# A hybrid attention and Fourier encoder layer: weight folds on another engine, one maximum for all late weights, squares and norms in another order

## The chip, the core and the metric

The kernel runs on one core of a Trainium2 chip. The core has five engines that run side by side, each through its own instructions in order: TensorE (PE, with its weight loads PEld), VectorE (DVE), ScalarE (ACT), GpSimd (POOL) and SyncE (SP, which here only issues DMA transfers). The metric is the device time of one launch in microseconds, the median over several runs.

## The reference, cut to what matters

One encoder layer, applied with the same weights to two requests (`prompt`, `sample`) of 2048 tokens with 1024 features:

```python
u = _rmsnorm(h, g_norm)
q, k, v, ga, f, gf = split(u @ w_in)          # 512, 128, 128, 512, 512, 512 columns
q = rope(_rmsnorm(q, g_q)); k = rope(_rmsnorm(k, g_k))        # per head of 64
a  = softmax(q k^T / 8) v * silu(ga)          # 8 query heads, 2 key/value heads, all tokens
fo = (Re(fft2(f)) per group of 64 channels, @ w_fmix) * silu(gf)
h = h + concat(a, fo) @ w_out
gate = sigmoid(_rmsnorm(h, g_ple) @ w_ple_gate)
y = _rmsnorm(h + (p @ w_ple) * gate, g_final)
```

All of it is float32. The kernel multiplies in float16, each operand split in a high and a low half, three products for one.

## The kernel before, in words

**Stages.** First the projections (`project`): x is read in 32 tiles of 128 rows, two tiles to a step, so 16 steps or chunks, 8 for each request. A row tile is scaled by its inverse norm, split in halves and transposed by DMA to `uc`. From it come q and kv (`mm_tile`), and, in the "sweep" of the chunk, f, gf and ga (`sweep_f`, `sweep_ga`). Then attention with the second half of the Fourier branch and the output projections beside it; the change does not touch the instructions of that stage, except for the order in which its first inputs are loaded and the place of its first maxima.

**The order of work is written out by hand.** Each engine gets its instructions in the order in which the program emits them. `iteration(i)` is the body of the projection: at its top the stores of the iteration before, then squares of the rows of chunk i+3 (`sq_u`, ACT, line 640, into `jk`), squares of z (q and k as projected) of chunk i-1 (`square_z`), the low halves of q of chunk i-3 (`lo_q`), the rotary product of chunk i-2 (`rope_q`), and `newton`: one inverse square root on DVE for q's norms of chunk i-1 and the row norms of chunk i+2 together (`rsqrt`, lines 269 to 284). Then the first row tile of chunk i, then the sweep of chunk i-1 in pieces (`sweep_part(us)` emits sweep steps until so many microseconds of PE work are spent). Between the pieces stand `fold_u`, `fold_s` (POOL, lines 811 and 817) and `fold_hl` (ACT and DVE, lines 824 and 825), which add and subtract the two row tiles of a chunk so that one matmul group does for both; behind the sweep stand `norm_q` (POOL, lines 627, 729 and 734), the high and low halves of u of chunk i+2 (`hi_u`, `lo_u`, and the transposes, line 481), the second half of the x loads for chunk i+4 (`load_x`, line 633, into 5 buffers), `hi_q` and the second row tile of chunk i.

**In a sweep**, f goes to PSUM, ACT copies it to `ft` (line 1004), and PE multiplies it by the first Fourier matrix (line 1009) between the two groups of gf. The results of gf, ga and the transform are stored by DMAs that POOL issues (lines 1052, 1071, 1018).

**Weights.** `weights` prepares the columns of q, kv, f, gf and ga at the start: load, maximum of each slice (DVE, line 349), maximum over the partitions (POOL, `partition_all_reduce`, line 359), a power of two as the factor, then the high and low halves (ACT and DVE, lines 371 and 372). For f, `fold_cols` first folds the columns of each of the 8 slices (POOL, lines 324 to 326). `weight_far` does the same for the weights of the output stage, six blocks, one after the other, with the halves going to DRAM; it runs as a background job, one turn for every five sweep steps (`bg`), and is followed in that job by `embed_rows`, which prepares p, and `channel_map`.

**The start of attention.** `early()`, at the end of iteration 13, loads the first k, v and q; `leads` then computes the first score maxima (lines 1325 and 1333), one turn for every five sweep steps.

Of the kernel before, what the change touches and what calls it, by code (L numbers as in the profile page):

```python
# [165 lines left out]
class Build:  # L166
# [151 lines left out]

    def fold_cols(self, w):

        g = self.nc.gpsimd
        e = w[:, :EVEN].rearrange("p (h c) -> p h c", c=33)[:, :, 1:32]
        o = w[:, EVEN:].rearrange("p (h c) -> p h c", c=31)
        g.tensor_tensor(out=e, in0=e, in1=o, op=ALU.add)
        g.tensor_scalar(out=o, in0=o, scalar1=-2.0, scalar2=None, op0=ALU.mult)
        g.tensor_tensor(out=o, in0=o, in1=e, op=ALU.add)

    def weights(self, blocks, stage, ahead):

        nc, st = self.nc, self.st
        sl = {}

        def load(i):
            if i < 8 * len(blocks):
                _, src, cols, _, _ = blocks[i // 8]
                sl[i] = stage(i % 8, cols)
                nc.sync.dma_start(sl[i], src[i % 8 * 128:(i % 8 + 1) * 128, :])
                if blocks[i // 8][0] == "f":  # L340
                    self.fold_cols(sl[i])

        for i in range(ahead):
            load(i)
            yield "loaded" if i == 7 else 0.0
        for b, (name, src, cols, g, dest) in enumerate(blocks):
            mx = st.tile([128, 8], F32, name="w_mx")
            for k in range(8):
                nc.vector.tensor_reduce(out=mx[:, k:k + 1], in_=sl[8 * b + k], op=ALU.max, axis=AX.X,
                                        apply_absolute_value=True)  # L350
                yield 0.0
            if g is not None:
                m2 = st.tile([128, 8], F32, name="w_m2")
                nc.vector.tensor_tensor(out=m2[:], in0=mx[:], in1=g[:], op=ALU.mult)
                mx = m2
            m1 = st.tile([128, 1], F32, name="w_m1")
            nc.vector.tensor_reduce(out=m1[:], in_=mx[:], op=ALU.max, axis=AX.X, apply_absolute_value=True)
            mm = st.tile([128, 1], F32, name="p2_mm")
            nc.gpsimd.partition_all_reduce(mm[:], m1[:], 128, bass_isa.ReduceOp.max)
            yield 0.0  # L360
            s, i = self.pow2_all("w_" + name, mm, W_EXP)
            self.sc[name] = i
            if g is not None:
                gs = st.tile([128, 8], F32, name="w_gs")
                nc.vector.tensor_scalar(out=gs[:], in0=g[:], scalar1=s[:], scalar2=None, op0=ALU.mult)
            dest = dest()
            yield 0.0
            for k in range(8):
                w = sl.pop(8 * b + k)
                f = gs[:, k:k + 1] if g is not None else s[:]  # L370
                nc.scalar.activation(dest[:, 0, k, :], w, AF.Copy, scale=f)  # L371
                nc.vector.scalar_tensor_tensor(out=dest[:, 1, k, :], in0=w, scalar=f, in1=dest[:, 0, k, :],  # L372
                                               op0=ALU.mult, op1=ALU.subtract)
                del w
                load(8 * b + k + ahead)
                yield "split" if k == 7 else 0.0

    def weight_far(self, name, src, cols, g, pool):

        nc, st = self.nc, self.st  # L380
        sl, ahead, nk = {}, AH, src.shape[0] // 128

        def load(j):
            if j < 2 * nk:
                sl[j] = pool.tile([128, 512], F32, name="w_st", tag="w2k", bufs=self.nw2k)
                nc.sync.dma_start(sl[j][:, :cols], src[j % nk * 128:(j % nk + 1) * 128, :])

        for j in range(ahead):
            load(j)
            yield  # L390
        mx = st.tile([128, 8], F32, name="w_mx")
        for k in range(nk):
            load(k + ahead)
            self.defer(lambda w=sl.pop(k), k=k: nc.vector.tensor_reduce(
                out=mx[:, k:k + 1], in_=w[:, :cols], op=ALU.max, axis=AX.X, apply_absolute_value=True))
            yield
        f = [None] * nk
        mm = st.tile([128, 1], F32, name="p2_mm")

        def scale():  # L400
            m = mx
            if g is not None:
                m = st.tile([128, 8], F32, name="w_m2")
                nc.vector.tensor_tensor(out=m[:], in0=mx[:], in1=g[:], op=ALU.mult)
            m1 = st.tile([128, 1], F32, name="w_m1")
            nc.vector.tensor_reduce(out=m1[:], in_=m[:, :nk], op=ALU.max, axis=AX.X, apply_absolute_value=True)
            nc.gpsimd.partition_all_reduce(mm[:], m1[:], 128, bass_isa.ReduceOp.max)

        def factors():
            s, self.sc[name] = self.pow2_all("w_" + name, mm, W_EXP)  # L410
            f[:] = [s[:]] * nk
            if g is not None:
                gs = st.tile([128, 8], F32, name="w_gs")
                nc.vector.tensor_scalar(out=gs[:], in0=g[:], scalar1=s[:], scalar2=None, op0=ALU.mult)
                f[:] = [gs[:, k:k + 1] for k in range(nk)]

        self.defer(scale)
        self.wd[name] = nc.dram_tensor("wd_" + name, (128, 2, nk, cols), F16, kind="Internal").ap()
        for _ in range(2):
            yield  # L420
        self.defer(factors)
        yield
        for k in range(nk):
            load(k + nk + ahead)
            w = sl.pop(k + nk)
            o = pool.tile([128, 2, 512], F16, name="w_o", tag="w2k", bufs=self.nw2k)
            nc.scalar.activation(o[:, 0, :cols], w[:, :cols], AF.Copy, scale=f[k])

            def low(k=k, w=w, o=o):
                nc.vector.scalar_tensor_tensor(out=o[:, 1, :cols], in0=w[:, :cols], scalar=f[k], in1=o[:, 0, :cols],  # L430
                                               op0=ALU.mult, op1=ALU.subtract)
                nc.sync.dma_start(self.wd[name][:, :, k, :], o[:, :, :cols])

            self.defer(low)
            yield

    def embed_rows(self, pool):
# [166 lines left out]
    def project(self, P, PU, W, early, later, wkv, wq, wf, wgf, wga, bg, mid):  # L604
# [241 lines left out]
        def iteration(i):  # L846
# [6 lines left out]
            for f in stores:  # L853
                f()
            del stores[:]
            if ok(i + 3):
                sq_u(i + 3)
            sq = square_z(i - 1) if ok(i - 1) else None
            if ok(i - 1) and i > 2:
                VL.pop((i - 1, 1))()  # L860
# [9 lines left out]
            if ok(i):  # L870
                sweep_part(4.0)
                VL.pop((i, 0))()
            if folds(i):
                sweep_part(1.5)
                fold_u(i, 0)
                fold_s(i, 0)
                fold_u(i, 1)
                sweep_part(8.0)
                fold_hl(i, 0)
                fold_s(i, 1)  # L880
                sweep_part(8.0)
                fold_hl(i, 1)
            sweep_part(1000.0 if i < n else (6.0, 9.0, 5.0, 100.0)[i - n])
            if ok(i - 1):
                norm_q(i - 1, rs)
            if ok(i + 2):
                hi_u(i + 2)
                for tt in range(CH):
# [5 lines left out]
            if ok(i):  # L894
                mm_tile(i, 1)
                append(i)
            if i == n - 3:
                early()
            if i == n:
# [67 lines left out]
        for f in stores_next:  # L967
            f()
        del stores_next[:]
        sq_u(3)  # L970
        sweep_part(11.6)
        mid()
        fold_u(1, 0)
        make_u(3, 0)
        load_x(5, 1)
        sq_u(4)
        fold_s(1, 0)
        fold_u(1, 1)
        sweep_part(3.0)
        fold_hl(1, 0)  # L980
        fold_s(1, 1)
        sweep_part(6.0)
        fold_hl(1, 1)
# [265 lines left out]
    def attention(self, kvp):  # L1249
# [7 lines left out]
        kt, vt, Q, P, O, MX, ACC, AT, M4, S, MR, AR = ({} for _ in range(12))  # L1257

        def load_kv(s, kv):
            for b in range(2):  # L1260
                k = kvp.tile([128, 4, 3, 128], F16, name=f"k{kv}", bufs=2)
                for h in range(2):
                    nc.sync.dma_start(k[:, 2 * h:2 * h + 2], self.kTd[s][kv][:, 4 * b + 2 * h:4 * b + 2 * h + 2])
                kt[s, kv, b] = k
            if s or not kv:
                load_v(s, kv)

        def load_v(s, kv):
            for b in range(2):
# [123 lines left out]

        self.kvp = kvp
        for kv in range(2):
            load_kv(0, kv)
            load_q(kv)
        nm = kvp.tile([128, 4, 128], F16, name="nm", bufs=1)
        nc.gpsimd.memset(nm[:], 0.0)
        kone = kvp.tile([128, 128], F16, name="kone", bufs=1)  # L1400
# [8 lines left out]
                negate(v - 1)  # L1409

        def leads():
            for g in range(-AHEAD, 0):
                yield from lead(g)
                yield
# [403 lines left out]
    def run(self):  # L1818
# [5 lines left out]
        with pool("psA", 5, space=PSUM) as self.psX, pool("A", side="right") as A:  # L1824
            with pool("A1", side="right") as A1:
# [58 lines left out]
                                   places([("uc", 3, 4), ("qs", 1, 2)] + [("qT", 2, 1)] * 2), 8)  # L1884

                def rest():
                    for n in range(2):
                        c = slice(n * 512, (n + 1) * 512)
                        yield from self.weight_far(f"wo{n}", a["w_out"][0][:, c], 512, None, A1)
                        yield from self.weight_far(f"pg{n}", a["w_ple_gate"][0][:, c], 512, self.gp, A1)  # L1890
                        yield from self.weight_far(f"wp{n}", a["w_ple"][0][:, c], 512, None, A1)
                    yield from self.embed_rows(A1)
                    yield from self.channel_map(A1)
                    self.scales3()
# [117 lines left out]
```

## Time and profile before

| | us |
|---|---|
| median of 3 runs | 2737.63 (2734.76 to 2737.71) |
| the profiled execution | 2728.66, span 2726.9 |
| granted PE clock, mean over the span | 0.974 |
| PE busy | 2536.3 (93%) |
| DVE busy | 1745.7 (64%) |
| ACT busy | 1182.6 (43%) |
| POOL busy | 1920.6 (70%) |
| projections, from the start to the first scores of attention | 863.7 |

How to read a row of the groups or the timeline: start and busy time, engine, line of the kernel, operation, output and inputs by the program's names, shape, count; in brackets the idle time of the engine before it and what ended it. A row of the waits gives the total, the number and the longest of the waits of one engine and line for another. "issue" as a releaser means that the profile shows nothing that the engine waited for. A name followed by q (SPq) is the engine's queue, which issues DMAs.

### The profile page before, as it was taken

How to read it: one execution, taken by the hardware profiler on the slowest of the kernel's cores; microseconds unless marked ns; L12 is line 12 of the kernel's file. 1: busy time of each engine (PE TensorE's matmuls, PEld its weight loads, DVE VectorE, ACT ScalarE, POOL GpSimd, SP SyncE). 2: the span in 40 equal slices, each digit the busy share in tenths (PEclk: the TensorE clock that was granted, in tenths of full speed). 3: DMA queues.
4: the chain of work that ended last, by engine and by line, in shares of the span. 5: the costliest groups of instructions: out<-in, count | busy, mean ns of one | idle time of the engine just before them, and what ended most of it. 6: DMA issues, size and time to landing. Idle time of an engine off the chain costs nothing. (4 is left out here: it accounts for less than half of the span.)

```text
span 2726.9 us, 49881 instructions
## 1 busy us (share of the span) xinstructions
PE 2536.3 (93%) x19896; PEld 1377.5 (51%) x19896; DVE 1745.7 (64%) x2326; ACT 1182.6 (43%) x1983; POOL 1920.6 (70%) x1598
## 2 busy tenths in 40 slices
PE   3898999979897999999999999999999999999998
PEld 1465656556555654444445454544444445544543
DVE  4767766767865675666566566665665566666634
ACT  2434324333322544544444445444444444544442
POOL 3255553545535996888788788888887887888870
PEclk7999999989898999999999999999999999999999
DMA  5646657657636762223232324322322222232223
GB/s 140 178 123 180 190 148 207 171 136 167 176 115 188 244 207 81 69 57 69 67 78 48 81 54 99 100 67 57 77 70 74 71 64 79 69 88 73 70 53 85
DMA packets 450601, 297.92 MB, mean 109 GB/s; under 512 B 294000, under 2 KB 394736, under 8 KB 450368
## 3 DMA queue, kind: packets, MB, share of 16 engines
q1 hardware_dynamic: 438512, 257.00, 36.9%
q0 software_dynamic: 11856, 37.74, 3.8%
q8 instruction: 155, 2.54, 0.4%
q14 instruction: 78, 0.64, 0.1%
HBM read 146.12 MB, written 82.45 MB: 84 GB/s over the span
## 5 line engine op out<-in xcount | busy, mean ns | idle before, releaser
L1303 POOL TENSOR_TENSOR acc<-acc,p 128x1024 f32<-128x1024 f32 x384 | 928.4, 2418 | 140.8 <-ACT p L1298 108.6
L1333 DVE TENSOR_REDUCE a_mx<-ps_m 128x1 f32<-128x1024 f32 x498 | 608.9, 1223 | 558.3 <-PE ps_m L1325 547.6
L1298 ACT ACTIVATE p<-ps_s,s_scale 128x512 f32<-128x512 f32 x1024 | 648.0, 684 | 668.1 <-PE ps_s L1295 650.9
L1619 PE MATMUL ps_g<-w_pg,hT 64*128 64x512 f16 x2784 | 494.9, 376 | 0.5 <-DVE h L1545 0.5
L1361 PE MATMUL ps_o<-p,v 128*64 128x256 f32 x4096 | 468.5, 382 | 0.0
L1295 PE MATMUL ps_s<-q,k 64*128 64x512 f16 x3072 | 435.7, 377 | 14.5 <-ACT p L1298 14.1
L488 PEld LDWEIGHTS <-uc 128*128 128x128 f16 x2400 | 239.8, 100 | 267.3 <-issue 64.0
L1361 PEld LDWEIGHTS ps_o<-p,v 128*64 128x64 f32 x4096 | 283.9, 137 | 160.0 <-issue 28.3
L1619 PEld LDWEIGHTS <-hT 64*128 64x128 f16 x2784 | 203.9, 94 | 156.4 <-issue 11.6
L1619 PE MATMUL ps_g<-w_wo,mh 64*128 64x512 f16 x1440 | 260.0, 376 | 13.7 <-DVE mh L1529 12.4
L1295 PEld LDWEIGHTS <-k 64*128 64x128 f16 x3072 | 151.9, 94 | 214.6 <-issue 93.5
L1619 PE MATMUL ps_g<-w_wo,mT 64*128 64x512 f16 x1440 | 259.2, 378 | 1.1 <-DMA mT<-mh 1.1
L1325 PE MATMUL ps_m<-k,q 64*128 64x512 f16 x996 | 201.2, 377 | 14.4 <-DVE a_mx L1333 14.4
L1301 POOL TENSOR_TENSOR acc<-p,p 128x1024 f32<-128x1024 f32 x64 | 150.9, 2358 | 25.6 <-ACT p L1298 24.8
L488 PEld LDWEIGHTS <-w_ga 128*128 128x128 f16 x1536 | 148.9, 98 | 26.5 <-DVE w_ga L372 3.7
L1619 PEld LDWEIGHTS <-mh 64*128 64x128 f16 x1440 | 100.6, 94 | 104.8 <-DVE mh L1529 17.6
L1619 PEld LDWEIGHTS <-mT 64*128 64x128 f16 x1440 | 103.7, 94 | 82.7 <-issue 5.1
L488 PE MATMUL ps_x<-w_gf,uc 128*128 128x512 f16 x552 | 135.0, 404 | 0.0
L1071 POOL DMA_DIRECT2D agd<-gat x64 | 35.4, 553 | 115.4 <-DVE gat L1081 104.1
L488 PE MATMUL ps_x<-wr_q,uc 128*128 128x512 f16 x384 | 88.0, 387 | 29.7 <-ACT wr_q L371 29.5
L488 PE MATMUL ps_x<-uc,w_ga 128*128 128x256 f16 x1008 | 113.5, 273 | 0.0
L1384 DVE RECIPROCAL ps_f<-ps_f 128x256 f32<-128x256 f32 x61 | 107.1, 1756 | 9.1 <-PE ps_f L1377 9.1
(342 smaller groups left out, 3464.0 us busy)
## 6 DMA issues: line engine op xcount, KB each, us to landing
q<-qTd SPq DMA_DIRECT2D x256, 64.0 KB, 2.3
ag<-agd SPq DMA_DIRECT2D x64, 256.0 KB, 3.2
out<-h POOLq DMA_DIRECT2D x31, 512.0 KB, 3.0
x<-in_x_prompt SPq DMA_DIRECT2D x16, 512.0 KB, 4.9
gfd<-gt POOLq DMA_DIRECT2D x32, 256.0 KB, 3.1
w_st<-in_w_out SPq DMA_DIRECT2D x32, 256.0 KB, 4.0
agd<-gat POOLq DMA_DIRECT2D x64, 128.0 KB, 2.8
w_st<-in_w_ple_gate SPq DMA_DIRECT2D x32, 256.0 KB, 3.7
```

The lines of the kernel that those rows point to most:

```text
L488: self.nc.tensor.matmul(ps, lhs(ia, k), rhs(ib, k), start=(i == 0), stop=(i == 3 * ks - 1))
L1071: nc.gpsimd.dma_start(self.agd[s][1, r * 128:(r + 1) * 128, c * n:(c + 1) * n], gt[:, :n])
L1295: nc.tensor.matmul(S[u][e][:], w[sl], q[sl].rearrange("p h q -> p (h q)"), start=j == i == 0, stop=i + 1 == len(todo), skip_group_check=True)
L1298: nc.scalar.activation(p[:, e, :], S[u][e][:], AF.Exp, scale=self.sc["s_scale"][:])
L1301: nc.gpsimd.tensor_tensor(out=ACC[u][:], in0=P[u, 0][:], in1=p[:], op=ALU.add)
L1303: nc.gpsimd.tensor_tensor(out=ACC[u][:], in0=ACC[u][:], in1=p[:], op=ALU.add)
L1325: nc.tensor.matmul(ps[c], Q[u][0][sl, h, :], kt[s, kv, half][sl, :, 0, :], start=True, stop=True)
L1333: nc.vector.reduce_max(MX[u][:, h, half, c:c + 1], x, axis=AX.X)
L1361: nc.tensor.matmul(o[64 * f:64 * f + 64], vt[s, kv, c // 8][:, c % 8, :], p[:, e, f], start=(c == 0), stop=(c == 15))
L1384: nc.vector.reciprocal(r, r)
L1619: nc.tensor.matmul(g[0][:], g[1](ia, k)[sl], g[2](ib, k)[sl], start=a, stop=z, skip_group_check=True)
```

## The change

Six edits, made together:

- `fold_cols` runs on VectorE, with two instructions for a slice instead of three, and is called just before the maximum of the slice and not when the slice is loaded.
- Behind ga's maximum over partitions GpSimd gets one small addition, whose result is not used.
- The six calls of `weight_far` become one `weights_far`: the maxima of all 36 slices first, one maximum over partitions for six columns, then all 36 splits.
- `sq_u(i+3)` moves from the top of `iteration(i)` to its end.
- `norm_q(i-1)` moves from behind the sweep to ahead of u's folds; the pieces of the sweep between them change a little. In the part before the loop, the first half of chunk 1's fold moves ahead of the squares and of `mid`.
- The first k and q tiles are loaded ahead of v, and `leads` waits four turns before it begins.

```diff
     def fold_cols(self, w):
-        g = self.nc.gpsimd
+        g = self.nc.vector
...
         g.tensor_tensor(out=e, in0=e, in1=o, op=ALU.add)
-        g.tensor_scalar(out=o, in0=o, scalar1=-2.0, scalar2=None, op0=ALU.mult)
-        g.tensor_tensor(out=o, in0=o, in1=e, op=ALU.add)
+        g.scalar_tensor_tensor(out=o, in0=o, scalar=-2.0, in1=e, op0=ALU.mult, op1=ALU.add)
...
     def weights(self, blocks, stage, ahead):
...
-                if blocks[i // 8][0] == "f":
-                    self.fold_cols(sl[i])
...
             for k in range(8):
+                if name == "f":
+                    self.fold_cols(sl[8 * b + k])
                 nc.vector.tensor_reduce(out=mx[:, k:k + 1], in_=sl[8 * b + k], op=ALU.max, axis=AX.X,
...
             nc.gpsimd.partition_all_reduce(mm[:], m1[:], 128, bass_isa.ReduceOp.max)
+            if name == "ga":
+                nc.gpsimd.tensor_tensor(out=m1[:], in0=m1[:], in1=mm[:], op=ALU.add)
...
-    def weight_far(self, name, src, cols, g, pool):
+    def weights_far(self, specs, pool):
...
+        for j in range(AH):
+            load(j)
+            yield
+        mx = pool.tile([128, n, 8], F32, name="w_mxs", bufs=1)
+        nc.vector.memset(mx[:], 0.0)
+        for j, (w, k) in enumerate(slices):
+            load(j + AH)
+            nc.vector.tensor_reduce(out=mx[:, w, k:k + 1], in_=sl.pop(j)[:], op=ALU.max, axis=AX.X,
+                                    apply_absolute_value=True)
+            yield
...
+        nc.vector.tensor_reduce(out=m[:], in_=mx[:], op=ALU.max, axis=AX.X, apply_absolute_value=True)
+        nc.gpsimd.partition_all_reduce(mm[:], m[:], 128, bass_isa.ReduceOp.max)
+        for _ in range(6):
+            yield
...
+        for j, (w, k) in enumerate(slices):
+            load(j + len(slices) + AH)
+            x = sl.pop(j + len(slices))
+            o = pool.tile([128, 2, 512], F16, name="w_o", tag="w2k", bufs=self.nw2k)
+            nc.scalar.activation(o[:, 0, :], x[:], AF.Copy, scale=f[w, k])
+            nc.vector.scalar_tensor_tensor(out=o[:, 1, :], in0=x[:], scalar=f[w, k], in1=o[:, 0, :],
+                                           op0=ALU.mult, op1=ALU.subtract)
+            nc.sync.dma_start(self.wd[specs[w][0]][:, :, k, :], o[:])
             yield
...
         def iteration(i):
...
-            if ok(i + 3):
-                sq_u(i + 3)
             sq = square_z(i - 1) if ok(i - 1) else None
...
                 sweep_part(4.0)
                 VL.pop((i, 0))()
+                sweep_part(4.0)
+            if ok(i - 1):
+                norm_q(i - 1, rs)
             if folds(i):
-                sweep_part(1.5)
                 fold_u(i, 0)
                 fold_s(i, 0)
                 fold_u(i, 1)
                 sweep_part(8.0)
                 fold_hl(i, 0)
                 fold_s(i, 1)
-                sweep_part(8.0)
+                sweep_part(7.0)
                 fold_hl(i, 1)
             sweep_part(1000.0 if i < n else (6.0, 9.0, 5.0, 100.0)[i - n])
-            if ok(i - 1):
-                norm_q(i - 1, rs)
...
                 mm_tile(i, 1)
                 append(i)
+            if ok(i + 3):
+                sq_u(i + 3)
...
+        fold_u(1, 0)
+        fold_s(1, 0)
+        sweep_part(5.8)
+        fold_hl(1, 0)
         sq_u(3)
-        sweep_part(11.6)
+        sweep_part(5.8)
         mid()
-        fold_u(1, 0)
         make_u(3, 0)
+        fold_u(1, 1)
         load_x(5, 1)
         sq_u(4)
-        fold_s(1, 0)
-        fold_u(1, 1)
-        sweep_part(3.0)
-        fold_hl(1, 0)
         fold_s(1, 1)
         sweep_part(6.0)
         fold_hl(1, 1)
...
         for kv in range(2):
-            load_kv(0, kv)
+            load_k(0, kv)
             load_q(kv)
+        load_v(0, 0)
...
         def leads():
+            for _ in range(4):
+                yield
             for g in range(-AHEAD, 0):
```

More of the change, by code (lines that the diff above doesn't have):

```diff
@@ L376, in weights @@
                 yield "split" if k == 7 else 0.0
-    def weight_far(self, name, src, cols, g, pool):
+    def weights_far(self, specs, pool):
         nc, st = self.nc, self.st
-        sl, ahead, nk = {}, AH, src.shape[0] // 128
+        n = len(specs)
+        slices = [(w, k) for w, (_, src, _) in enumerate(specs) for k in range(src.shape[0] // 128)]
+        sl = {}
         def load(j):
-            if j < 2 * nk:
+            if j < 2 * len(slices):
+                w, k = slices[j % len(slices)]
@@ L385, in load @@
                 sl[j] = pool.tile([128, 512], F32, name="w_st", tag="w2k", bufs=self.nw2k)
-                nc.sync.dma_start(sl[j][:, :cols], src[j % nk * 128:(j % nk + 1) * 128, :])
-        for j in range(ahead):
+                nc.sync.dma_start(sl[j][:], specs[w][1][k * 128:(k + 1) * 128, :])
+        for j in range(AH):
             load(j)
             yield
[L391 to L395, printed above, removed]
+        mx = pool.tile([128, n, 8], F32, name="w_mxs", bufs=1)
@@ L396, in weight_far @@
+        nc.vector.memset(mx[:], 0.0)
[3 more added lines that the diff above has]
+                                    apply_absolute_value=True)
             yield
[L397 to L401, printed above, removed]
+        for w, (_, _, g) in enumerate(specs):
             if g is not None:
[L403 to L407, printed above, removed]
@@ L409, in factors @@
-        def factors():
-            s, self.sc[name] = self.pow2_all("w_" + name, mm, W_EXP)
-            f[:] = [s[:]] * nk
-            if g is not None:
[L413 to L418, printed above, removed]
@@ L419, in weight_far @@
-        for _ in range(2):
-            yield
-        self.defer(factors)
+                nc.vector.tensor_tensor(out=mx[:, w], in0=mx[:, w], in1=g[:], op=ALU.mult)
+        m, mm, p = [st.tile([128, n], F32, name=f"wf_{x}", bufs=1) for x in ("m", "mm", "p")]
+        nc.vector.tensor_reduce(out=m[:], in_=mx[:], op=ALU.max, axis=AX.X, apply_absolute_value=True)
+        nc.gpsimd.partition_all_reduce(mm[:], m[:], 128, bass_isa.ReduceOp.max)
+        for _ in range(6):
+            yield
+        s, i = self.keep("wf_s", [128, n]), self.keep("wf_i", [128, n])
@@ new lines, in weights_far @@
+        nc.vector.tensor_scalar(out=p[:], in0=mm[:], scalar1=1e-30, scalar2=None, op0=ALU.max)
+        nc.vector.tensor_scalar(out=p[:].bitcast(I32), in0=p[:].bitcast(I32), scalar1=0x7F800000,
+                                scalar2=None, op0=ALU.bitwise_and)
+        nc.vector.tensor_scalar(out=s[:].bitcast(I32), in0=p[:].bitcast(I32), scalar1=-1,
+                                scalar2=(254 + W_EXP) << 23, op0=ALU.mult, op1=ALU.add)
+        nc.vector.tensor_scalar(out=i[:], in0=p[:], scalar1=2.0 ** -W_EXP, scalar2=None, op0=ALU.mult)
@@ new lines, in weights_far @@
+        f = {}
+        for w, (name, src, g) in enumerate(specs):
+            self.sc[name] = i[:, w:w + 1]
+            nk = src.shape[0] // 128
+            self.wd[name] = nc.dram_tensor("wd_" + name, (128, 2, nk, 512), F16, kind="Internal").ap()
+            for k in range(nk):
+                f[w, k] = s[:, w:w + 1]
+            if g is not None:
+                gs = pool.tile([128, 8], F32, name="w_gs8", bufs=2)
+                nc.vector.tensor_scalar(out=gs[:], in0=g[:], scalar1=s[:, w:w + 1], scalar2=None, op0=ALU.mult)
+                for k in range(nk):
+                    f[w, k] = gs[:, k:k + 1]
@@ L422, in weight_far @@
         yield
-        for k in range(nk):
-            load(k + nk + ahead)
-            w = sl.pop(k + nk)
+        for j, (w, k) in enumerate(slices):
+            load(j + len(slices) + AH)
+            x = sl.pop(j + len(slices))
             o = pool.tile([128, 2, 512], F16, name="w_o", tag="w2k", bufs=self.nw2k)
[L427 to L434, printed above, removed]
+            nc.scalar.activation(o[:, 0, :], x[:], AF.Copy, scale=f[w, k])
+            nc.vector.scalar_tensor_tensor(out=o[:, 1, :], in0=x[:], scalar=f[w, k], in1=o[:, 0, :],
+                                           op0=ALU.mult, op1=ALU.subtract)
+            nc.sync.dma_start(self.wd[specs[w][0]][:, :, k, :], o[:])
@@ L1259, in load_kv, with load_k @@
         def load_kv(s, kv):
+            load_k(s, kv)
+            load_v(s, kv)
+        def load_k(s, kv):
             for b in range(2):
@@ L1264, in load_kv @@
                 kt[s, kv, b] = k
-            if s or not kv:
-                load_v(s, kv)
         def load_v(s, kv):
@@ L1886, in rest @@
                 def rest():
[L1887 to L1891, printed above, removed]
+                    c = [slice(n * 512, (n + 1) * 512) for n in range(2)]
+                    yield from self.weights_far([x for n in range(2) for x in (
+                        (f"wo{n}", a["w_out"][0][:, c[n]], None), (f"pg{n}", a["w_ple_gate"][0][:, c[n]], self.gp),
+                        (f"wp{n}", a["w_ple"][0][:, c[n]], None))], A1)
                     yield from self.embed_rows(A1)
```

## The prediction

> **What bounds the kernel now.** First the busy time by stretch, then what TensorE (PE) waited for, then the timeline at those waits. In windows: length, busy time of PE, PEld, DVE, ACT, POOL, then the granted clock.
>
> ```profile
> 128.00:149.00 21.00, 8.84 (x51) 6.16 (x52) 9.70 (x19) 6.97 (x13) 16.73 (x15) 0.67 0.67 180
> 150.00:700.00 550.00, 508.98 (x3343) 331.47 (x3341) 400.74 (x701) 197.56 (x346) 282.91 (x232) 0.96 0.61 163
> 700.00:865.00 165.00, 138.51 (x866) 84.99 (x865) 118.81 (x236) 43.63 (x83) 76.95 (x70) 0.90 0.57 151
> ```
>
> Attention starts at about 864 and its instructions are not edited, so everything is decided before. There PE is the bound, with holes: 12.2 us in the first window (21.00 - 8.84), 41.0 in the second, 26.5 in the third. The waits of the first 1000 us name them, and a larger one at the start (total, times, longest):
>
> ```profile
> PE ps_x L488 <- ACT wr_q L371: 29.5, 1, 29.5
> PE ps_f L1009 <- ACT ft L1004: 16.5, 3, 7.2
> PE ps_g L1009 <- ACT ft L1004: 15.5, 1, 15.5
> PE ps_x L1325 <- DVE a_mx L1333: 13.1, 2, 6.7
> PE ps_g L1036 <- ACT uf L824: 11.2, 1, 11.2
> PE ps_x L1325 <- DMA q<-qTd: 10.7, 1, 10.7
> PE ps_x L1009 <- ACT ft L1004: 9.1, 2, 5.9
> ```
>
> The three ft rows are 41.1: all the idle time of 150 to 700. The Fourier transform (L1009) needs ft, and ACT is late with it. The timeline shows why, in program order:
>
> ```profile
> 232.96 4.70 SPq L481 DMA_TRANSPOSE uc<-hl  x2
> 237.71 0.96 SPq L633 DMA_DIRECT2D x<-in_x_prompt  x1
> 242.13 1.06 ACT L640 ACTIVATE jk<-x 128x1024 f16<-128x1024 f32 x1 [8.22 <-DMA x<-in_x_prompt]
> 245.28 0.70 ACT L1004 ACTIVATE ft<-ps_g,inv_f 128x512 f32<-128x512 f32 x1
> 246.04 2.08 PE L1009 MATMUL ps_f<-ft,dft 128*128 128x512 f32 x2 [7.24 <-ACT ft L1004]
> 247.91 4.29 PE L488 MATMUL ps_x<-w_gf,uc 128*128 128x512 f16 x10
> 640.02 1.02 PE L1009 MATMUL ps_x<-ft,dft 128*128 128x512 f32 x2
> 640.88 5.34 PE L488 MATMUL ps_x<-w_gf,uc 128*128 128x512 f16 x24
> ...
> 682.55 1.02 PE L1009 MATMUL ps_g<-ft,dft 128*128 128x512 f32 x2
> ```
>
> SP issues the row load at 237.71, once its transposes are out; ACT's next instruction squares those rows and stands 8.22 us; all of ACT's evacuations stand behind it. PE then starts cold: 2.08 against 1.02 for the transform, and 4.29 for ten matmuls that take 2.2 warm (5.34 x 10/24), so 3.1 us on top of the hole.
>
> **The change, part by part.**
>
> *Squares at the iteration's end.* `sq_u(i+3)` moves past everything ACT has in iteration i. Its rows were loaded at the end of iteration i-1, a whole iteration (over 40 us) earlier. It issues no DMA.
>
> ```profile
> ACT jk L640 <- DMA x<-in_x_sample: 61.0, 8, 11.1
> ACT jk L640 <- DMA x<-in_x_prompt: 12.4, 2, 8.2
> ACT uf L824 <- POOL f_s L817: 32.0, 8, 10.2
> ```
>
> Between 150 and 700 that takes 73.4 us of standing out of ACT. What it leaves behind: two squares of 1.06 in front of the squares of z, ready rows, nothing late. Worth on PE: the 41.0 of holes and the cold starts. Five holes at about 3 us each are 14, so 55 is there. An undisturbed chunk, transform to transform, is 42.5 us of back-to-back PE (640.02 to 682.55), so no other engine forbids it: DVE's 400.74 of 550 and POOL's 282.91 leave room.
>
> *norm_q before u's folds.* Now POOL folds u while DVE's Newton steps run, and `norm_q` follows at the end, beside DVE's split of u:
>
> ```profile
> 7.46 0.18 DVE L274 TENSOR_TENSOR rsq_t<-rsq_y 128x22 f32<-128x22 f32 x1
> 571.43 0.71 POOL L627 TENSOR_TENSOR rt<-rt,g_q_t 128x256 f32<-128x256 f32 x1 [7.48 <-issue]
> 572.91 2.33 POOL L729 TENSOR_TENSOR qn<-z,q_rs 128x1280 f32<-128x1280 f32 x1
> 575.32 3.47 POOL L734 TENSOR_TENSOR t<-qn,rt 128x1024 f32<-128x1024 f32 x2
> 583.86 2.06 DVE L274 TENSOR_TENSOR rsq_t<-rsq_y 128x22 f32<-128x22 f32 x1
> 593.25 0.91 ACT L468 ACTIVATE p_hl<-p_in,p_f 128x256 f16<-128x256 f32 x2 [15.57 <-DVE p_f L463]
> ```
>
> An operation of 0.18 takes 2.06 beside POOL's fold, and the wait of 15.57 behind it made the 15.5 hole. After the change POOL cannot start `qn` before Newton ends, so Newton runs free. In exchange folds queue behind 7.2 us (0.71 x 2 + 2.33 + 3.47), and the gfd, gd and agd stores POOL issues stand behind both. My estimate from these rows and the order of instructions, counted from the end of PE's previous row tile: squares and sums to 8, Newton to 12, norm_q to 18, f_t and f_s to 23; ACT reaches its first uf at about 25 (8 of row tile, 16 of sweep). About 2 us of slack. If that goes, the row above says what covers it: ACT waited for f_s eight times, up to 10.2, and PE never for that in 150 to 700, since its banks are ahead. SP: the rope load, issued at an iteration's top, is now needed some 25 us sooner, but still after Newton.
>
> *One maximum over partitions.* Six all-reduces become one; each made POOL switch code, 7.48 us before L627 after one of them (row above) and as much in front (5.98 below). Five less free POOL of some 65 us (5 x 13.5), and its norm_q at 571.43 comes on time. The same 72 loads and 36 stores stay; the background job has 21 turns fewer (102 to 81), so p's loads and transposes reach SP about 105 sweep steps (five to a turn), over one chunk, sooner, and no longer share DVE with attention's first maxima. The one switch left may cost one iteration up to 10; inside the term.
>
> Of these 55 I take 47: ACT keeps waits on weight loads and one switch. Bounds 30 (half of the cold starts and a third of holes come back as other waits) and 57.
>
> *f's columns on DVE.* Here the start:
>
> ```profile
> 29.29 0.19 DVE L659 TENSOR_SCALAR n_ms<-n_su 128x2 f32<-128x2 f32 x1 [2.70 <-ACT jk L640]
> 53.23 0.38 POOL L359 PARTITION_ALL_REDUCE p_mm<-w_m  x1 [5.98 <-issue]
> 54.48 2.56 ACT L371 ACTIVATE wr_q<-w_z,w_gs 128x512 f16<-128x512 f32 x4 [25.22 <-DVE w_gs L365]
> 107.19 0.50 PE L488 MATMUL ps_f<-uc,w_ga 128*128 128x256 f16 x3 [0.39 <-DVE w_ga L372]
> 129.37 0.41 DVE L1081 SCALAR_TENSOR_TENSOR gat<-th,ps_f 128x256 f32<-128x256 f32 x1
> ```
>
> q's all-reduce stands behind 24 fold instructions on POOL. Without them q's factor waits only for DVE's Newton: 29.29, twelve steps to 31.6, factor to 32.4; ACT starts 22 us earlier. DVE takes over 8 x 2 operations of 248 columns at 0.45 (the 256-column row, and a gap): 7.2 us, ahead of f's, gf's and ga's factors. From 85 to 112 PE already runs at DVE's and ACT's pace (the wait at 107.19), so I charge 5 to 6: 16 to 17 earlier at 112.
>
> *First folds earlier, an add behind ga's all-reduce.*
>
> ```profile
> 124.58 2.12 POOL L811 TENSOR_TENSOR f_t<-uc 128x1024 f32<-128x1024 f16 x1 [7.00 <-DVE q_rs L670]
> 135.38 2.48 POOL L817 TENSOR_TENSOR f_s<-f_t 128x512 f32<-128x512 f32 x2
> ```
>
> The 7.00 has q_rs as its releaser, which f_t does not read: it is the switch back, and the add makes POOL pay it early. Half 0 is folded early; half 1 still follows norm_q(0), and ACT's squares now wait for half 0's buffer. By my count the hole shortens by at most 5 and Newton starts 4 later: nothing net. Start: -17, bounds -8 and -28 (the whole second hole too).
>
> [...]
>
> *Loads of k and q ahead of v; attention's maxima four turns later.*
>
> ```profile
> 728.13 2.37 SPq L1281 DMA_DIRECT2D q<-qTd  x4
> 733.13 0.28 ACT L717 ACTIVATE vs<-ps_g 128x128 f32<-128x128 f32 x1 [16.10 <-DMA vd<-vs]
> 785.28 0.58 PE L1325 MATMUL ps_x<-k,q 64*128 64x512 f16 x1 [6.74 <-DVE a_mx L1333]
> 857.09 1.70 SPq L784 DMA_DIRECT2D qTd<-qT  x2
> 863.70 0.39 PE L1295 MATMUL ps_s<-mr,kone 64*128 64x512 f16 x2
> ```
>
> The 10.7 on q goes (20 sweep steps later), but SP issues 18 DMAs as before ahead of vd, so ACT's 16.10 stays and PE stops at the next transform instead: -6 (0 to -10). Behind the 6.74 is Newton beside folds: -8 with its cold start (0 to -10). The last chunk hangs on a chain through DVE, POOL and SP's stores at 857.09, and the transposed maxima of unit 0 now queue behind those: 0 (+5 to -8).
>
> Sum: -47 - 17 - 6 - 8 = -78. The profiled execution took 2728.66 (span 2726.9), the median 2737.63, 9 more; I take the sum off the median: **2660**.
>
> **Rivals.**
> - *The standing moves.* ACT drops the x wait and stands at others (vd, w_st, p_f), as at 733.13; half of steady gain and nothing at the second stage: -24 - 17 = -41, 2697. For: ACT has such waits now. Against: PE ignored them.
> - *Contention moves.* Newton gets free, but norm_q and the folds slow other DVE work just before ACT needs it: the 15.5 and 6.7 holes with their cold starts stay, about 25 less: -53, 2685. [...]
> - *Everything works*, second hole and tail too: -105, 2633.
> - *Folds late (slower).* norm_q in front delays f_s; each of 14 iterations stops ACT at uf. PE is covered to 10.2. It decides from a delay of 16 us on, 6 us of PE a time: 14 x 6 = 84 against 78, 2744. My count has f_s 2 us early, so the delay would have to come from elsewhere.
> - *No effect:* PE's holes are bought back by DVE's extra load, within 0.2% (5.5 us, about what a measurement here can tell), 2737.
>
> **Chances.** Forecast 0.55; standing moves 0.16; contention moves 0.12; everything 0.08; slower 0.05; no effect 0.04. Faster 0.91, same 0.04, slower 0.05. Range: the forecast's bounds with contention and most of the moved standing, 2637 to 2697.
>
> **What would show it.** PE's first wr_q matmul near 33; one all-reduce after 110; no ACT wait for x after 150, and none of ft over 4 us between 150 and 700; Newton steps of 0.2; ACT's wait for vd near 14 still there; attention's first scores near 786. Wrong would be: PE waits for ft of the old size with another releaser on ACT, or uf as a releaser of PE's waits in every chunk.

## The result and the profile after

The changed kernel takes 2663.26 us (median of 4 runs, 2659.65 to 2668.79) and the kernel before, measured beside it, 2736.20 (4 runs, 2731.13 to 2737.71). The ratio, taken from all the runs and not from the medians, is 0.9738 with a 95% interval of 0.9716 to 0.9761: 73 us faster by the medians, where 78 were forecast. One execution of a variant below (no_add), 6438.22 us at a granted clock of 0.399, is left out of its time and its ratio. The profiled execution of after took 2668.79, its span is 2667.0 and its clock 0.984 (0.974 before). It is the longest of its four, and before's profiled one (2728.66) is shorter than the four runs of that kernel above. So the two traces differ by only 60, and a step read from them is good to a few us.

The windows of after (same columns as before's; the first is the hole ahead of the first folded group, the last ends with attention's first scores):

```profile
110.00:131.00 21.00, 4.39 (x31) 3.02 (x29) 14.79 (x35) 7.92 (x12) 13.47 (x10) 0.64 0.50 118
150.00:700.00 550.00, 530.06 (x3493) 346.90 (x3491) 387.65 (x746) 218.43 (x378) 284.80 (x245) 0.98 0.71 187
700.00:802.00 102.00, 94.77 (x626) 59.45 (x624) 66.70 (x143) 25.55 (x47) 45.82 (x44) 0.95 0.39 108
```

Between 150 and 700 PE idles 19.9 us (550.00 - 530.06) instead of 41.0. PE's waits in the first 1000 us of after, the largest seven:

```profile
PE ps_x L491 <- DMA uc<-hl: 18.4, 1, 18.4
PE ps_g L1039 <- ACT uf L827: 16.4, 1, 16.4
PE ps_x L491 <- ACT wr_q L372: 7.7, 1, 7.7
PE ps_x L556 <- DMA wfm<-in_w_fmix: 7.4, 1, 7.4
PE ps_f L1012 <- ACT ft L1007: 7.3, 2, 5.8
PE ps_m L1330 <- DVE a_mx L1338: 6.3, 8, 2.6
PE ps_x L1330 <- DVE a_mx L1338: 4.6, 1, 4.6
```

The 29.5 on wr_q is 7.7, the ft waits fell from 41.1 to 12.6 (7.3 here, and 3.4 and 1.9 in smaller rows), and the 10.7 on q is gone. Two rows grew or are new: 16.4 on uf (11.2 before) and 7.4 on wfm. The 18.4 at the head is no new hole: it is the time until PE's first matmul, which was 17.7 before, with wr_kv as its releaser. ACT's waits between 150 and 700:

```profile
ACT th L1082 <- PE ps_x L491: 64.0, 19, 10.4
ACT p_hl L471 <- DVE p_f L466: 54.5, 13, 9.0
ACT vs L720 <- DMA vd<-vs: 46.1, 9, 8.0
ACT uf L827 <- POOL f_s L820: 19.0, 6, 10.1
```

The wait for x, 73.4 before, is not there. ACT now waits most for PE itself, which is where one wants it. The wait for vd's store was 2.3 in this window before, and 16.10 once behind it; now nine waits make 46.1.

By stage, from the starts of the transform's first matmuls in both traces (chunk numbers as in the prediction):

| stage | before, us | after, us | difference | forecast |
|---|---|---|---|---|
| start of the span to chunk 1's transform | 153.56 | 138.72 | -14.8 | -17 |
| chunk 1 to chunk 12 | 528.99 | 492.83 | -36.2 | -47 |
| chunk 12 to 13 | 56.66 | 57.32 | +0.7 | -6 |
| chunk 13 to 14 | 55.07 | 44.68 | -10.4 | -8 |
| chunk 14 to 15 | 42.45 | 40.06 | -2.4 | 0 |
| chunk 15 to attention's first scores | 26.97 | 27.16 | +0.2 | 0 |
| attention to the end of the span | 1863.2 | 1866.2 | +3.0 | 0 |

### The profile page after: what moved, and what is told of

It reads as the page before. It is cut to its first block, busy times and chain, and to the rows that moved or that the text cites. A ratio compares the mean times of both kernels' runs of the same rounds, so it can differ in the third digit from the quotient of the medians.

```text
span 2667.0 us, 49778 instructions
## 1 busy us (share of the span) xinstructions
PE 2530.7 (95%) x19896; PEld 1376.4 (52%) x19896; DVE 1695.7 (64%) x2318; ACT 1186.3 (44%) x1983; POOL 1885.7 (71%) x1570
## 3 DMA queue, kind: packets, MB, share of 16 engines
q8 instruction: 155, 2.54, 0.4%
## 5 line engine op out<-in xcount | busy, mean ns | idle before, releaser
L1300 PE MATMUL ps_s<-q,k 64*128 64x512 f16 x3072 | 436.6, 378 | 15.1 <-ACT p L1303 14.8
L1366 PEld LDWEIGHTS ps_o<-p,v 128*64 128x64 f32 x4096 | 283.9, 137 | 160.1 <-issue 28.5
L754 POOL TENSOR_TENSOR t<-t,t 128x1280 f32<-128x1280 f32 x16 | 46.3, 2891 | 123.3 <-DVE t L750 123.3
L491 PE MATMUL ps_x<-w_gf,uc 128*128 128x512 f16 x552 | 129.2, 391 | 0.8 <-DVE w_gf L373 0.4
```

The lines of the kernel that those rows point to most:

```text
L491: self.nc.tensor.matmul(ps, lhs(ia, k), rhs(ib, k), start=(i == 0), stop=(i == 3 * ks - 1))
L754: nc.gpsimd.tensor_tensor(out=t1[:], in0=t1[:], in1=t2[:], op=ALU.add)
L1300: nc.tensor.matmul(S[u][e][:], w[sl], q[sl].rearrange("p h q -> p (h q)"), start=j == i == 0, stop=i + 1 == len(todo), skip_group_check=True)
L1366: nc.tensor.matmul(o[64 * f:64 * f + 64], vt[s, kv, c // 8][:, c % 8, :], p[:, e, f], start=(c == 0), stop=(c == 15))
```

## The experiments

Twelve kernels ran. Besides the time, one number is compared below: from chunk 1's transform to chunk 12's ("the stretch"), and from there to chunk 15's ("the end"). The stretch is 492.8 in the changed kernel and 490.4 and 492.4 in two variants of it that take about as long (no_add, back_lead), so single traces agree within some 2 us. Ratios are to the kernel before.

**The three parts that act in the steady iterations, each alone on the kernel before and each taken out of the changed kernel.** The edits are one part of the diff forwards or backwards:

```diff
 # only_sq: before, with this; back_sq: after, with the reverse
-            if ok(i + 3):
-                sq_u(i + 3)
             sq = square_z(i - 1) if ok(i - 1) else None
...
                 append(i)
+            if ok(i + 3):
+                sq_u(i + 3)
 # only_norm: before, with this; back_norm: after, with the reverse
+                sweep_part(4.0)
+            if ok(i - 1):
+                norm_q(i - 1, rs)
             if folds(i):
-                sweep_part(1.5)
...
-                sweep_part(8.0)
+                sweep_part(7.0)
...
-            if ok(i - 1):
-                norm_q(i - 1, rs)
 # only_far: before, with this; back_far: after, with the reverse
-                        yield from self.weight_far(...)  # six blocks, an all-reduce each
+                    yield from self.weights_far([...], A1)  # one all-reduce of six columns
```

> The changed kernel with the squares of the rows of chunk i+3 put back at the top of the iteration; all else as changed. Theory A (ACT standing at the x load makes the holes before the Fourier transforms): ACT waits for x again, some 60 us in total between 140 and 700, PE's waits for ft rise from 27 to 45 us or more, and the time rises by 25 to 40 us, to about 2695. Theory B (the holes came from Newton's steps beside POOL's folds and from the all-reduces, and the wait for x only stood in front): ACT waits for x, but the time rises by less than 10.

> The kernel before with only the squares moved to the iteration's end. Theory A: ACT no longer waits for x, the holes at the transforms shrink from 41 to under 20 us, and the time falls by 25 to 40, to about 2705. Theory B: it falls by less than 10, since Newton still runs beside the folds and the six all-reduces stay.

> The changed kernel with norm_q behind the sweep again and the old pieces of the sweep. Theory A: Newton's squaring steps are back at 1 to 2 us beside the folds and DVE is late now and then, which costs 5 to 12. Theory B: the holes come back, 25 or more.

> The changed kernel with the late weights prepared one block after the other, six maxima over partitions, as before. Theory A: six switches of POOL of about 13 us each, two or three of which meet norm_q or a fold that ACT needs: 5 to 15 more, and the background job ends 21 turns later, so that p's rows meet attention's first maxima. Theory B: 15 or more. That POOL's idle time hides it all: within 4.

> The kernel before with norm_q(i-1) moved alone, in the iterations only: ahead of the folds, with the changed kernel's sweep pieces. Undone from the changed kernel, this move cost 17 us, of it 14.5 between the transforms of chunks 1 and 12. Theory 1 (each part takes away one of several lateness of the same ACT and DVE stream, and nothing shows until a second is gone, as with the squares alone, which gave 0): within 4 us of the kernel before; PE's ft waits between 150 and 700 stay near 40, ACT waits for x (jk) as before, since the squares still stand at the top of the iteration. Rival (the parts add up, and only the squares need norm_q): 14 to 20 faster than the kernel before, ft waits near 25.

> The kernel before with weights_far alone (one generator over six blocks, one all-reduce of six columns, no deferred reductions) and nothing else of the change. Undone from the changed kernel it cost 20 us, 17 of it between the transforms of chunks 1 and 12. Theory 1 (nothing shows until a second part is there): within 5 us of the kernel before, ft waits between 150 and 700 near 40, the waits of DVE on POOL's all-reduces (p2_mm) gone from the list all the same. Rival (the parts add up): 15 to 20 faster, first transform of chunk 12 at 663 to 668 instead of 682.6.

| kernel | parts in it | time, us | ratio [95%] | stretch | end |
|---|---|---|---|---|---|
| before | none | 2731 to 2736 | 1 | 529.0 | 154.2 |
| only_sq | squares | 2733.55 | 1.0001 [0.9988, 1.0015] | 532.3 | 151.4 |
| only_norm | norm_q | 2718.68 | 0.9952 [0.9936, 0.9967] | 528.7 | 142.9 |
| only_far | one maximum | 2700.33 | 0.9890 [0.9874, 0.9905] | 508.8 | 144.6 |
| back_far | squares, norm_q | 2682.99 | 0.9811 [0.9786, 0.9837] | 509.7 | 143.9 |
| back_norm | squares, one maximum | 2680.18 | 0.9808 [0.9785, 0.9831] | 507.3 | 141.5 |
| back_sq | norm_q, one maximum | 2681.01 | 0.9809 [0.9784, 0.9834] | 508.2 | 140.4 |
| after | all three | 2663.26 | 0.9738 [0.9716, 0.9761] | 492.8 | 142.1 |

(The last four also have the change's other parts: their start is some 15 us shorter, and their end has the new order of loads.) Two rows that differ in one part give its worth in the stretch. One maximum is worth 17 to 25 whatever else is there (529.0 - 508.8, 532.3 - 507.3, 528.7 - 508.2, 509.7 - 492.8). The squares without norm_q are worth -3 to 2, with it 15 to 19; norm_q without the squares 0 to 1, with them 14 to 23; the pair 16 (508.8 - 492.8) to 19 (529.0 - 509.7). The end falls by some 10 as soon as norm_q is early or the six all-reduces are gone, and the second of these adds little there. That is why each part taken out of the changed kernel costs 14 to 17 in the stretch, 47 in all (17 to 20 and 54 in time), more than the 36 that the three gave there: whoever takes out one of the pair loses the other as well.

Why the squares alone gave nothing is in ACT's waits between 150 and 700 of only_sq:

```profile
ACT z L715 <- POOL qn L729: 39.6, 8, 10.3
ACT uf L824 <- POOL f_s L817: 35.3, 8, 10.3
ACT vs L717 <- DMA vd<-vs: 29.3, 6, 7.0
```

The wait for x is gone, as in after. But ACT then comes to `z`, whose buffers are free only when POOL has done the late norm_q of the chunk before: 39.6 us there (7.4 before) and 29.3 at vd (2.3 before), for the 73.4 that left. PE's ft waits are 45.2, not less than 41.1. ACT's timeline shows the new wait ahead of ft:

```profile
340.04 0.28 ACT L717 ACTIVATE vs<-ps_x 128x128 f32<-128x128 f32 x1 [6.89 <-DMA vd<-vs]
437.44 0.60 ACT L715 ACTIVATE z<-ps_x 128x512 f32<-128x512 f32 x1 [5.42 <-POOL qn L729]
439.47 0.69 ACT L1004 ACTIVATE ft<-ps_g,inv_f 128x512 f32<-128x512 f32 x1
```

Of the six holes ahead of a transform, five had the wait for x as the last long wait of ACT in the kernel before. In only_sq four of these five have the one at vd and one, here at 437.44, the one at z. The sixth and largest (15.49 before, 15.31 here) stands in both kernels behind the wait of `p_hl` for `p_f`. With norm_q alone, ACT still waits for x, and also for folds that now stand behind norm_q on POOL:

```profile
ACT uf L824 <- POOL f_s L817: 60.6, 10, 14.6
ACT jk L640 <- DMA x<-in_x_sample: 60.1, 8, 12.3
```

PE's ft waits are 40.6 there. Newton's steps run free in only_norm (the median of line 274's first step is 0.18, in the kernel before 2.06) and the stretch does not move; in only_far they are still slow (2.06) and it falls by 20. So free Newton steps by themselves give the stretch nothing. Whether they, or z's buffer, make norm_q worth 14 to 23 once the squares are out of the way is not separated.

With one maximum alone, the wait for x stays almost whole (ACT, then PE):

```profile
ACT jk L642 <- DMA x<-in_x_sample: 56.1, 8, 10.8
ACT uf L826 <- POOL f_s L819: 19.3, 5, 9.9
PE ps_x L1011 <- ACT ft L1006: 11.3, 2, 8.3
PE ps_g L1011 <- ACT ft L1006: 9.9, 1, 9.9
PE ps_f L1011 <- ACT ft L1006: 4.5, 2, 3.5
```

PE's ft waits fell to 25.7 all the same. What left the lists were rows of before: DVE's waits for the all-reduces and for norm_q's result, and ACT's for the factors behind the all-reduces; and uf's wait shrank from 32.0:

```profile
DVE p_p L298 <- POOL p_mm L407: 24.4, 5, 7.7
DVE t L747 <- POOL qn L729: 28.6, 4, 10.6
ACT w_o L427 <- DVE w_wo_s L303: 27.2, 2, 15.7
```

So of the two theories that stood for single parts, "nothing until a second part is there" holds for norm_q in the stretch and fell for one maximum (30 us faster, chunk 12's transform at 664.28), and "the parts add up" the other way round. only_norm's 13 us are nearly all in the end (154.2 to 142.9), which neither theory had in view. Not separated: whether it is the five all-reduces or the reductions that no longer wait in the deferred queue, since weights_far does both.

**The start.**

```diff
 # back_fold: after, f's columns folded on POOL when loaded
 # no_add: after, without
-            if name == "ga":
-                nc.gpsimd.tensor_tensor(out=m1[:], in0=m1[:], in1=mm[:], op=ALU.add)
 # back_lead: after, attention's maxima at once
         def leads():
-            for _ in range(4):
-                yield
 # fold11: after, in the filling stage
         make_u(3, ...)                     # without norm_q(0) in it
         fold_u(1, 1)
...
         fold_s(1, 1)
+        norm_q(0, rs)
```

> The changed kernel with f's columns folded by POOL at the load again, three instructions for a slice. My theory: q's maximum over partitions stands behind 24 instructions and a switch, PE's first wr_q matmul goes from 34 back to about 55, and of these 21 us about 15 stay at the first transform of chunk 1, because DVE is relieved of 7 and the hole before the folded f group shrinks by itself: 13 to 18 more. Rival (DVE's chain sets the start whatever POOL does): within 5.

> The changed kernel without the small addition behind ga's maximum over partitions. If POOL begins its switch back when the next compute instruction comes to the head of its queue, the fold of chunk 1 is that instruction now and stands there early: POOL's f_t starts within 1 us of 95.4 and the time stays within 3. If the switch begins only when the inputs of that instruction are ready, f_t starts near 100 and the time rises by up to 4, most of it hidden behind norm_q, since the hole is set by the second half.

> The changed kernel with attention's first maxima starting at once, the loads in the new order. My theory: the first maxima stand in front of the q load again and PE waits for it some 5 to 10 us in chunk 13; ACT's wait for vd hides part of it: 2 to 6 more. Rival (SP's 18 loads hold ACT up anyway and PE waits there instead): within 2.

> The changed kernel with norm_q(0) emitted after fold_s(1,1) in the filling stage instead of between make_u(3) and fold_u(1,1), so POOL's second pair of folds (f_t at 122.9, f_s at 125.1) starts before t (118.08, 4.87 long) instead of behind it. Theory (the hole of 16.4 ahead of the folded f group is POOL's order: fold pair behind q's norm): the hole shrinks by 5 to 9, the first transform at 130 to 134 instead of 138.7, the time 4 to 9 below the changed kernel, if the Newton step's result that is 5 later delays nobody. Rival (the hole moves: ACT's second fold part or qn for chunk 0 is late instead): the first transform within 2 of 138.7 or the gain given back by chunk 2, the time within 3.

| kernel | time, us | ratio [95%] | chunk 1's transform | stretch |
|---|---|---|---|---|
| after | 2663.26 | 0.9738 [0.9716, 0.9761] | 138.72 | 492.8 |
| back_fold | 2675.41 | 0.9785 [0.9764, 0.9806] | 156.80 | 487.4 |
| no_add | 2665.01 | 0.9744 [0.9723, 0.9765] | 139.00 | 490.4 |
| back_lead | 2662.34 | 0.9742 [0.9721, 0.9763] | 136.89 | 492.4 |
| fold11 | 2662.16 | 0.9746 [0.9727, 0.9765] | 133.85 | 490.7 |

The fold on DVE is the whole start: without it the transform is 18.1 later, of which 5.4 come back in the stretch, and 12 remain. The add and the four turns are worth nothing that shows. POOL's timeline, first of after, then of no_add, tells why the add is idle:

```profile
86.36 0.35 POOL L358 PARTITION_ALL_REDUCE p_mm<-w_m  x1 [18.55 <-DVE w_m L356]
95.27 0.18 POOL L360 TENSOR_TENSOR w_m<-w_m,p_mm 128x1 f32<-128x1 f32 x1 [8.55 <-issue]
95.42 2.11 POOL L814 TENSOR_TENSOR f_t<-uc 128x1024 f32<-128x1024 f16 x1
```
```profile
87.15 0.35 POOL L358 PARTITION_ALL_REDUCE p_mm<-w_m  x1 [18.55 <-DVE w_m L356]
95.72 2.11 POOL L812 TENSOR_TENSOR f_t<-uc 128x1024 f32<-128x1024 f16 x1 [8.22 <-DVE gt L1082]
```

What comes next on POOL stands behind the all-reduce either way, the add 8.55 and the fold 8.22 (the add 8.09 in back_lead and 7.73 in fold11). The six late all-reduces of the kernel before show the same: POOL idles 5.89 to 6.08 ahead of each and 6.86 to 9.46 ahead of the compute instruction behind each, and two MODIFY_POOL_CONFIG rows of its queue (POOLq) go with every one of these twelve holes; they are taken here as the start of a switch. In no_add the profile names DVE's gt as what the fold waited for, but the fold does not read it, and POOLq shows when the switch back began. The rows give the count, the shortest, median and longest in ns, and the first and last start; the first is after's, ahead of the add, the second no_add's, ahead of the fold:

```profile
L360 POOLq MODIFY_POOL_CONFIG  x2: 83/83/83, 86.7 to 86.7; - x2
L812 POOLq MODIFY_POOL_CONFIG  x2: 83/83/83, 87.4 to 87.5; - x2
```

Both stand right at the end of the all-reduce (86.71 and 87.50), and no_add's fold starts at 95.72, as the first of the two readings in its expectation had it (95.4) and not the second (near 100): in these traces the switch begins when the next compute instruction comes to the head of the queue. In the kernel before, the fold came there only behind POOL's DMA issues; its first such row is at 117.7, 6.9 ahead of the fold at 124.58. The changed order brings the fold up to where it pays early by itself.

fold11 took the hole of 16.4 down to 11.9, just less than the 5 to 9 that were expected, and its trace is 4.9 ahead at chunk 1's transform and 7.0 at chunk 12's. What was not seen ahead: f_s shares one buffer with ACT's squares, and in fold11 it stands 12.29 until those are done (it starts at 119.68). The median is that of after. With ranges of 9 us in after and 11 in fold11, whether the five are real in the time stays open.

**What holds PE next.** After's largest ft wait, with ACT and SP around it:

```profile
389.42 5.54 SPq L484 DMA_TRANSPOSE uc<-hl  x2
396.59 0.47 SPq L725 DMA_DIRECT2D vd<-vs  x1
401.68 0.28 ACT L720 ACTIVATE vs<-ps_x 128x128 f32<-128x128 f32 x1 [6.85 <-DMA vd<-vs]
403.08 0.67 ACT L1007 ACTIVATE ft<-ps_g,inv_f 128x512 f32<-128x512 f32 x1
403.81 2.07 PE L1012 MATMUL ps_f<-ft,dft 128*128 128x512 f32 x2 [5.76 <-ACT ft L1007]
```

vs has two buffers, the store that frees one stands on SP behind two transposes, and ft stands behind vs on ACT. And channel_map's matmul meets its weights too early:

```profile
647.08 0.66 SPq L547 DMA_DIRECT2D wfm<-in_w_fmix  x1
651.38 2.04 PE L556 MATMUL ps_x<-wfm,m 64*128 64x384 f32 x4 [7.41 <-DMA wfm<-in_w_fmix]
```

```diff
 # vs3
-            vs = P.tile([128, CH, 2, 64], F32, name="vs", bufs=2)
+            vs = P.tile([128, CH, 2, 64], F32, name="vs", bufs=3)
 # best: vs3, fold11, and in channel_map, after its loads
-        for _ in range(4):
+        for _ in range(10):
             yield
```

> The changed kernel with three buffers for v's values (vs) instead of two. ACT waits 46 us in 9 pieces for the store of vs between 130 and 700, since the store stands behind SP's transposes; PE's remaining waits for ft (12.5 us between 300 and 545, with cold starts some 19) stand behind one of these at 401.68. If that is their cause: ACT's wait is gone, the waits for ft fall under 4 and the time by 8 to 18. If the p rows and weight loads on ACT are: the time stays within 4.

> The changed kernel with three things: vs in three buffers (alone it gave 4.6), the fold order of the run before this one, and channel_map waiting ten turns of its generator instead of four, so that its matmul meets wfm after it has landed (PE waited 7.4 for it at 651). Theory: 4.6 plus 4 to 9 plus 4 to 7: 2645 to 2652, 1.004 to 1.008 times faster than the changed kernel. Rival (waits move on: with vs freed early, p_hl and w_o wait instead, and ten turns only push the start of attention's leads): 2655 to 2660, no better than vs alone.

vs3 took 2658.63 (0.9730 [0.9715, 0.9744]), best 2648.70 (0.9698 [0.9683, 0.9712]; 4 runs, 2646.05 to 2651.26). Best's interval lies under after's, each taken against the kernel before on its own chip: 0.9698/0.9738 is 0.996, some 11 us, so best beats both kernels, as its theory had it. vs3's interval overlaps after's, so what vs alone is worth in time is not settled; its median is 4.6 below after's, where its theory had 8 to 18. On the waits that theory was half right: three holes behind vd went (1.51, 1.89 and 5.76 in after, one of 2.54 in vs3), but PE's ft waits are 14.8 for 12.6, since the hole behind p_hl grew from 3.37 to 12.29. Best's stretch is 491.4, not shorter; its end is 130.3 instead of 142.1 (139.7 in vs3), so the gain is there, mostly channel_map's: no run has that part alone, but vs3 and fold11, with one of the other two parts each, have ends of 139.7 and 140.2. PE's and ACT's waits between 150 and 700 of best:

```profile
PE ps_g L1012 <- ACT ft L1007: 11.1, 1, 11.1
PE ps_f L1012 <- ACT ft L1007: 2.4, 1, 2.4
ACT p_hl L471 <- DVE p_f L466: 59.1, 11, 12.9
ACT w_o L434 <- DMA w_st<-in_w_out: 35.4, 6, 13.8
```

The vd wait is gone, and ACT stands longer at w_st instead (13.8 at most, 6.6 in after); PE's ft waits are 13.5 for 12.6, and the largest is behind p_hl as in vs3:

```profile
537.94 0.91 ACT L471 ACTIVATE p_hl<-p_in,p_f 128x256 f16<-128x256 f32 x2 [12.92 <-DVE p_f L466]
538.75 0.67 ACT L1007 ACTIVATE ft<-ps_x,inv_f 128x512 f32<-128x512 f32 x1
```

DVE works without a pause from 519.75 to 538 and comes to p_f only behind Newton's steps. It is the wait that the prediction showed with 15.57, and a candidate for a next step; no run here takes it away. The channel_map matmul runs without a wait, and at 1.13 instead of 2.04, the slower clock gone too (granted 0.50 from 651.3 to 660 in after, 1.00 from 669 to 676 in best):

```profile
670.03 1.13 PE L556 MATMUL ps_x<-wfm,m 64*128 64x384 f32 x4
```

## Why the prediction was right, step by step

The time (2663 for 2660) and the range held. Two things stand behind that agreement: the sum of the traces' steps is -60 and the medians' difference is -73, so part of it is where the profiled executions lie among their runs; and the terms erred in both directions, the stretch alone by 11. That the median came within 3 is in part luck.

- *Squares: the step that failed.* "Worth on PE: the 41.0 of holes and the cold starts" credited the largest wait in front of ft with all the holes behind it, the one of 15.5 too, which the next part put down to p_f. Alone the part gave 0 (1.0001): the rival "the standing moves" in full, at z and vd. It earns its 15 to 19 only with norm_q early.
- *norm_q before the folds.* The Newton steps did run free (line 274's first: 0.18 in the median instead of 2.06), and the price that was named, folds queued behind it, was real: uf waited 60.6 instead of 32.0 in only_norm, and 53.0 in back_far. PE was covered, as said: no wait on uf in 150 to 700. In the changed kernel it is 19.0, since the all-reduces no longer sit on POOL.
- *One maximum: under-sized as a cause.* The prediction gave it no amount of its own and spoke of POOL's time; it is worth 17 to 25 of the stretch, and the only part that works alone there. The three together were set at -47 within 30 to 57 and came out at -36. Of that, 28.5 is ft waits (41.1 to 12.6); the other 7.7 was not broken down, but two fewer transforms at the slow 2.08 (four in the kernel before, two in after), at 3.1 each, would be 6 of it; the reserve of 8 for waits that stay was too small by 11.
- *The start*, -17 foretold, -14.8 found. PE's first wr_q matmul is at 34.00 (33 foretold), ga's all-reduce comes 18.0 earlier (104.41 to 86.36). The hole ahead of the folded f group grew by 5 where "nothing net" was said: half 1's folds do follow norm_q(0), as the prediction said, but its t took 4.87, not the 3.47 that the prediction counted with. The prediction had the add as what pays POOL's way back; no_add shows that it is idle, because the way back is paid at the same place without it: 8.55 stand between the all-reduce and the add in after, 8.22 between it and the fold in no_add.
- *Chunk 13*, -6 foretold, +0.7 found. The q wait went, as said, and vd's 16.10 became 6. But the background job that is 21 turns shorter also brings channel_map forward, from the stage between chunks 14 and 15 (804.54 before, no wait, 1.13 for each of its two groups of matmuls) into this one. There it waits 7.41 for wfm, its two groups take 2.04 and 2.07, and the matmuls around them run slower too (granted clock 0.50). The prediction followed those 21 turns for p alone.
- *Chunk 14*, -8 foretold, -10.4 found, but not by the way that was named. The prediction put it down to Newton beside folds, which norm_q ends; one maximum alone gives all of it (44.68 in only_far), norm_q alone 7.5 (47.59 in only_norm), and back_far, with norm_q early and six all-reduces, only 2.6 (52.44). The -2.4 in the stage behind it is channel_map's two groups, which stood there before.
- *Signs named ahead.* Attention's first scores are at 800.77 in the profiled execution, not 786; in those of back_lead and best, 794.61 and 784.31. One ft wait is 5.76, where none over 4 was to be, and vd's wait near 14 is not there. The others came: Newton steps of 0.18, no wait of ACT for x after 150, and one all-reduce after 110 (at 280.49).

## What to carry to other kernels

The longest wait on the engine that is late is a candidate, not a price: ask what the engine meets next when that wait is gone, and whether that has been late all along behind it (here a buffer freed by a late step of another engine). Moves that each free one of two consecutive blockers can read 0 alone and a full gain together, so test them in pairs, too, before one is dropped. And when a background job becomes shorter, follow every item behind it, not only the one that was in view.

## What was not expected of the hardware

DVE's split of u, a two-operand pass over 128x1024, took 2.48 for two in fold11 with POOL standing idle, and 5.96 for the same two beside POOL's qn and t in after. This t took 4.87, where every later row of two in after took 3.02 to 3.37:

```profile
118.08 4.87 POOL L737 TENSOR_TENSOR t<-qn,rt 128x1024 f32<-128x1024 f32 x2
116.40 5.96 DVE L690 SCALAR_TENSOR_TENSOR hl<-x,rsq_z,hl 128x1024 f16<-128x1024 f32 x2 [0.81 <-ACT hl L681]
```
```profile
116.33 2.48 DVE L690 SCALAR_TENSOR_TENSOR hl<-x,rsq_z,hl 128x1024 f16<-128x1024 f32 x2 [0.81 <-ACT hl L681]
```

The prediction had such slowing for a small DVE operation (0.18 to 2.06); here both engines lose, DVE more than half its rate. In the kernel before, the same two took 3.98 in five chunks (at 230.50 for example, with POOL's rt and qn from 230.98 to 236.67), and in the changed kernel 2.47 or 2.48 in every chunk behind the first. only_norm has the short rows too, while back_norm has 3.73 to 3.98 in most chunks, so it is norm_q ahead of the folds that freed this pass; the prediction did not price that.
